# Seven-product quads: weight sums by accumulating transfers, seventeen quads, aligned operands

## The chip, the core and the metric

The program runs on one core of one Trainium2 chip. Its time is the device time in microseconds (us), the median of several runs. TensorE multiplies, ScalarE (ACT) and VectorE (DVE) work on elements, GpSimd (POOL) does a few small steps and can issue transfers, SyncE (SP) issues most transfers.

## What is computed

One layer of a hybrid block, on 256 rows of 2048 numbers in float32, with all the weights read from memory once:

```python
hn = rms_norm(x, norm_w)
proj = hn @ w_in                 # q, k, v, z_a, z_s, xbc, dt, g_a, g_s
o_a = dilated attention of q, k, v, times silu(z_a)
y = rms_norm(ssd scan of conv(xbc), times silu(z_s))      # 4096 wide
merged = sigmoid(g_a) * (o_a @ w_attn_branch) + sigmoid(g_s) * (y @ w_ssm_branch)
out = rms_norm(x + merged @ w_out)
```

The change touches two of these products: y @ w_ssm_branch (256 x 4096 by 4096 x 2048, called ssm) and the v part of hn @ w_in (256 x 2048 by 2048 x 2048, called v).

## The kernel before

Every product is made from two parts of each factor: a number is split into h, its value rounded to the matmul's format (ScalarE, a copy), and l, the rest (VectorE, a subtraction). Three matmuls xh*h, xh*l and xl*h are one full product; `triple` (lines 381 to 384) issues them. A matmul here has a 128 x 128 left block and 512 columns.

The weights lie in memory in the order of use, in units of 128 x 1024 numbers, 512 KB (`lay_weights`). SP loads a unit into one of four buffers w (`load`), ScalarE and VectorE split it into h and l, of which there are four buffers each (`unit`, lines 209 to 226), and TensorE multiplies. The tile framework sets the semaphores and, from a simulated timeline, the order on each engine and on SP's queue. A block under `high_priority(L_AHEAD)` is put ahead; loads are not in such a block. SP and POOL work their queues in order, and an instruction that waits for a buffer holds up what stands behind it.

The stages follow each other: the scan with its projections (pool ssm), then ssm and v (pool mul), then attention with q, k, za and the gates ga (pool att), then the attention branch and the output. ssm and v are made by `gemm_pair` (lines 373 to 449), each in two halves of 1024 columns (c = 0 and c = 2). A half runs over slots q of 256 rows of the weights: 16 in ssm, 8 in v. A plain slot multiplies 2 x 2 blocks of the left side with 2 x 2 blocks of the weights: 8 products, 24 matmuls. A *quad* (slots named in `S_QUADS`) makes the same from 7 products, 21 matmuls, in the manner of Strassen and Winograd: some products are of sums of blocks. For that the two units of a quad are laid out as (B11, B22) and (B12, B21). The seven are summed over all quads of a half in four extra PSUM banks, the prods; `fold` (lines 451 to 461) combines them, and they are added to the plain banks es. The second half swaps the roles of the eight banks.

In a quad VectorE makes t13 = (B12 - B11, B12 - B22) from both units (line 425), then two more sums in the place of B12 and B21 (lines 430 and 431). The parts of the units are named ha, la (of B11, B22) and hc, lc (of B21), those of the sums ht, lt (htt and ltt for t13, htu and ltu for the others in the profile). The left factors are sums too: `turn_x` (lines 351 to 364) adds h and l of a left block back together, makes four sums S and splits them into sx, 4 KB in each partition. It is called for all of ssm's quads before the first half (line 794), and the second half uses the same; for v it is called ahead of each half for the quads that are new.

The pools of SBUF are stacked: lead, big (the large left sides XT and yT), stream (w, h, l), ev (three pairs of 1 KB tiles for evacuating PSUM), const, and then one stage's pool after another at the same place. The pool mul now starts at byte 184192 of a partition, 384 past a multiple of 512. The memory of a stage's pool is free for the next when the last reader of what lay there is done.

Of the kernel before, what the change touches and what calls it, by code (L numbers as in the profile page):

```python
# [9 lines left out]
F32 = mybir.dt.float32  # L10
F32R = mybir.dt.float32r
AF = mybir.ActivationFunctionType
ALU = mybir.AluOpType
PSUM = bass.MemoryType.PSUM

P = 128
# [22 lines left out]
    ("ssm", 0): (3, 6, 9, 12), ("ssm", 2): (3, 6, 9, 12),  # L39
# [128 lines left out]
def hybrid_block(ctx: ExitStack, tc: tile.TileContext, wall, xt, x, pk_d, cst_d, fw_d, out):  # L168
# [6 lines left out]
    ev = ctx.enter_context(tc.tile_pool(name="ev", bufs=2))  # L175
# [175 lines left out]
    def turn_x(pool, x):  # L351

        sx = pool.tile([P, 2, 4, P], F32R, name=f"sx{now[0]}", tag="sx", bufs=4)
        tmp = pool.tile([P, 4, 512], F32, name=f"sxt{now[0]}", tag="tmp", bufs=1)
        a = tmp[:, 0].rearrange("p (k i s) -> p k i s", k=2, i=2)
        s = tmp[:, 1].rearrange("p (n s) -> p n s", n=4)
        xf = x.bitcast(F32)
        ve.tensor_tensor(a.rearrange("p k i s -> p k (i s)"), xf[:, :, :S], xf[:, :, S:], ALU.add)
        a11, a21, a12, a22 = a[:, 0, 0], a[:, 0, 1], a[:, 1, 0], a[:, 1, 1]
        ve.tensor_tensor(s[:, 0], a21, a22, ALU.add)  # L360
        ve.tensor_tensor(s[:, 1], a21, a11, ALU.subtract)
        ve.tensor_tensor(s[:, 2], s[:, 0], a11, ALU.subtract)
        ve.tensor_tensor(s[:, 3], a12, s[:, 2], ALU.subtract)
        split(s, sx[:, 0], sx[:, 1])
        return sx

    def gemm_pair(tag, pool, x_of, n_kt, sxs, swap, extra):

# [19 lines left out]
        for q in range(n_q):  # L388
# [32 lines left out]
            two = lambda t: t.rearrange("p (k m) -> p k m", k=2)  # L421
            with tc.high_priority(L_AHEAD):
                t13 = pool.tile([P, UNIT], F32, name=f"t13_{n}", tag="t13", bufs=1)
                b12 = wb[:, :512].unsqueeze(1).to_broadcast([P, 2, 512])
                ve.tensor_tensor(two(t13), b12, two(wa), ALU.subtract)
# [4 lines left out]
                ve.tensor_tensor(wb[:, :512], wa[:, 512:], t13[:, :512], ALU.subtract)  # L430
# [6 lines left out]
            sx = [(sx[:, 0, k], sx[:, 1, k]) for k in range(4)]  # L437
# [14 lines left out]
    def fold(prods, dst):  # L452

        d11, d12, d21, d22 = dst
        p1, p5, p6, p7 = prods
        ac.activation(d11, p1, AF.Copy)
        ac.activation(d22, p5, AF.Copy)
        ve.tensor_tensor(d12, p6, d11, ALU.add)
        ve.tensor_tensor(d21, p7, d12, ALU.add)
        ve.tensor_tensor(d12, d12, d22, ALU.add)  # L460
        ve.tensor_tensor(d22, d21, d22, ALU.add)
# [27 lines left out]
    rx = cpool.tile([P, S], F32, name="rx", tag="rx")  # L489
# [46 lines left out]
    dtT = cpool.tile([P, 2, SH], F32, name="dtT", tag="dtT")  # L536
    acT = cpool.tile([P, 2, SH], F32, name="acT", tag="acT")
    crT = cpool.tile([P, SH], F32, name="crT", tag="crT")
    acum_d = dram.tile([SH, S], F32, name="acum_d", tag="acum_d")

    with tc.tile_pool(name="ssm", bufs=2) as sp:
        def dt_sum(acc):
            hx, lx = dts[:, 6, :], dts[:, 7, :]
            ac.activation(hx, acc[:SH, S:], AF.Copy)
            ac.activation(lx, acc[SH:, :S], AF.Copy)
            ve.tensor_tensor(hx, acc[:SH, :S], hx, ALU.add)
            ve.tensor_tensor(hx, hx, lx, ALU.add)
# [159 lines left out]
        def find_r():  # L707
            part = cpool.tile([P, 4], F32, name="part", tag="part")
            for n in range(4):
                ac.activation(x_block(n), x_block(n), AF.Square, accum_out=part[:, n : n + 1])  # L710
            sums = cpool.tile([P, 2], F32, name="sums", tag="sums")
# [58 lines left out]
    with tc.tile_pool(name="mul", bufs=1) as sm:  # L770
        def scale_gate():
# [32 lines left out]
        sxs = {}  # L804
        for c in (0, 2):
            for q in S_QUADS[("v", c)]:
                if q not in sxs:
                    sxs[q] = turn_x(sm, XT[:, 2 * q : 2 * q + 2, :])
            es, prods = gemm_pair(("v", c), sm, lambda kt: XT[:, kt, :], KT, sxs, c == 2, {})
            dst = blocks(vt, c)  # L810
            fold(prods, dst)
            for d, e in zip(dst, es):
                ve.tensor_tensor(d, e, d, ALU.add)

    late = ctx.enter_context(tc.tile_pool(name="late", bufs=1))
    th_a = late.tile([P, 2, D], F32, name="th_a", tag="th_a")
    with tc.tile_pool(name="att", bufs=2) as ap:

# [145 lines left out]
```

## Time and profile before

| | us |
|---|---|
| median of 3 runs | 1409.14 (1409.02 to 1409.28) |
| the profiled execution | 1409.67 |
| its span, from the first to the last instruction | 1407.9 |
| ssm, from its first matmul to v's first | 586.0 to 756.7 |
| v, to the end of its last plain slot | 756.7 to 841.5 |
| TensorE busy in the span | 1395.6 |
| VectorE busy | 1005.2 |
| ScalarE busy | 782.6 |

How to read the rows below. A row of a timeline has start, duration, engine, line, operation, tiles written and read, form and count, and in brackets the idle time before it and what ended it. Matmuls are pipelined, so one starts before the one before it has ended: the step is the distance of two starts, not the duration. A row by stage has each engine's busy time and its count of instructions (those that overlap the edge are counted), then the granted clock, the share of the 16 DMA engines' time, and GB/s. A row on transfers has count, size of one, and median us from issue to landing. A row on waits has the total, the number of times and the longest.

### The profile page before, as it was taken

The numbers are of one execution on the slowest core, as the hardware profiler recorded it, in microseconds if no ns is written. First come the engines' busy times: TensorE is split into PE (matmuls) and PEld (weight loads), VectorE is DVE, ScalarE is ACT, GpSimd is POOL, SyncE is SP. The second block draws the span as 40 slices with busy tenths as digits, with TensorE's granted clock in tenths as the row PEclk, the third lists the DMA queues.
The fourth block names the chain that finished last, engine by engine and source line by source line (L and its number), as shares of the span: only waits on it lengthen the run. The fifth ranks groups of instructions, "written<-read, shape, count | busy, mean of one in ns | idle before, by whom it ended". The sixth has DMA issues, their size and how long they took to land.

```text
span 1407.9 us, 19734 instructions
## 1 busy us (share of the span) xinstructions
PE 1395.6 (99%) x7347; PEld 1184.9 (84%) x7347; DVE 1005.2 (71%) x1483; ACT 782.6 (56%) x1209; POOL 15.2 (1%) x66
## 2 busy tenths in 40 slices
PE   9999999999999999999999999999999999999997
PEld 7788888888888888888888888888888888888886
DVE  6988787776788797787777986666666654455654
ACT  7657577675668576665454554544444444444443
POOL 1000000000000000000000000000000000000000
PEclk9999999999999999999999999999999999999999
DMA  9666565656565665556556566555555557666663
GB/s 322 222 208 211 174 204 171 216 181 198 176 209 188 196 197 175 180 180 214 189 193 200 193 220 184 179 175 170 175 170 174 171 178 280 193 186 187 184 194 120
DMA packets 78208, 272.31 MB, mean 193 GB/s; under 512 B 8800, under 2 KB 9376, under 8 KB 77728
## 3 DMA queue, kind: packets, MB, share of 16 engines
q1 hardware_dynamic: 77392, 269.88, 60.9%
q8 instruction: 57, 0.93, 0.3%
q10 hardware_dynamic: 720, 1.18, 0.2%
q14 instruction: 39, 0.32, 0.1%
HBM read 268.86 MB, written 2.16 MB: 193 GB/s over the span
## 4 chain that ended last, share of the span: by engine, by line
PE 98%; DVE 1%; DMA 0%; SPq 0%; issue 0%; ACT 0%; POOLq 0%; DVEq 0%; POOL 0%
PE ps_zs L260 8%; PE ps_xs L260 8%; PE ps_za L260 4%; PE ps_k L260 4%; PE ps_q L260 4%; PE ps_zs L261 4%; PE ps_xs L261 4%; PE ps_ssm L382 4%; PE ps_ssm L383 4%; PE ps_ssm L384 3%; PE ps_q L261 2%; PE ps_k L261 2%; PE ps_za L261 2%; PE ps_attn L346 2%; PE ps_attn L347 2%; PE ps_attn L348 2%
## 5 line engine op out<-in xcount | busy, mean ns | idle before, releaser
L222 DVE TENSOR_TENSOR l<-w,h 128x1024 fp32r<-128x1024 f32 (+1 forms) x454 | 549.1, 1213 | 308.8 <-ACT h L221 306.0
L221 ACT ACTIVATE h<-w 128x1024 fp32r<-128x1024 f32 (+1 forms) x454 | 476.2, 1050 | 478.1 <-issue 92.5
L260 PE MATMUL ps_zs<-XT,h 128*128 128x512 f32 x496 | 176.2, 397 | 0.0
L260 PE MATMUL ps_xs<-XT,h 128*128 128x512 f32 x496 | 175.0, 395 | 0.0
L261 PE MATMUL ps_zs<-XT,l 128*128 128x256 f32 x496 | 139.4, 281 | 0.0
L261 PE MATMUL ps_xs<-XT,l 128*128 128x256 f32 x496 | 138.8, 280 | 0.0
L260 PEld LDWEIGHTS ps_zs<-XT,h 128*128 128x128 f32 x496 | 93.1, 188 | 22.7 <-issue 1.2
L260 PEld LDWEIGHTS ps_xs<-XT,h 128*128 128x128 f32 x496 | 93.0, 188 | 21.7
L261 PEld LDWEIGHTS ps_zs<-XT,l 128*128 128x128 f32 x496 | 93.6, 189 | 0.1
L261 PEld LDWEIGHTS ps_xs<-XT,l 128*128 128x128 f32 x496 | 93.6, 189 | 0.0
L260 PE MATMUL ps_q<-XT,h 128*128 128x512 f32 x256 | 92.3, 404 | 0.0
L260 PE MATMUL ps_za<-XT,h 128*128 128x512 f32 x256 | 89.6, 394 | 0.0
L260 PE MATMUL ps_k<-XT,h 128*128 128x512 f32 x256 | 89.6, 394 | 0.0
L383 PE MATMUL ps_ssm<-l,yT 128*128 128x512 f32 x192 | 74.9, 390 | 0.0
L384 PE MATMUL ps_ssm<-h,yT 128*128 128x512 f32 x192 | 74.6, 390 | 0.0
L382 PE MATMUL ps_ssm<-h,yT 128*128 128x512 f32 x192 | 72.4, 390 | 0.0
L261 PE MATMUL ps_q<-XT,l 128*128 128x256 f32 x256 | 71.2, 278 | 0.0
L261 PE MATMUL ps_za<-XT,l 128*128 128x256 f32 x256 | 71.0, 277 | 0.0
L261 PE MATMUL ps_k<-XT,l 128*128 128x256 f32 x256 | 71.0, 277 | 0.0
L260 PEld LDWEIGHTS ps_k<-XT,h 128*128 128x128 f32 x256 | 48.0, 188 | 11.2
L260 PEld LDWEIGHTS ps_za<-XT,h 128*128 128x128 f32 x256 | 48.0, 188 | 11.2
L260 PEld LDWEIGHTS ps_q<-XT,h 128*128 128x128 f32 x256 | 48.0, 188 | 10.9
(349 smaller groups left out, 2787.7 us busy)
## 6 DMA issues: line engine op xcount, KB each, us to landing
w<-in_wall SPq DMA_DIRECT2D x480, 512.0 KB, 3.7
acb<-acum_d SPq DMA_DIRECT2D x32, 256.0 KB, 3.6
th_s<-in_x SPq DMA_DIRECT2D x4, 512.0 KB, 7.5
fin<-in_x SPq DMA_DIRECT2D x1, 2048.0 KB, 9.4
early<-in_xt SPq DMA_DIRECT2D x7, 256.0 KB, 7.4
fw<-in_fw SPq DMA_DIRECT2D x1, 1024.0 KB, 11.5
out<-fin SPq DMA_DIRECT2D x4, 256.0 KB, 2.9
out<-fin ACTq DMA_DIRECT2D x4, 256.0 KB, 3.2
```

The costliest lines, as they stand in the source:

```text
L221: ac.activation(h[:, a:b], w[:, a:b], AF.Copy)
L222: ve.tensor_tensor(l[:, a:b], w[:, a:b], h[:, a:b].bitcast(F32), ALU.subtract)
L260: pe.matmul(acc, h[:, kk, :], m, start=(kt == 0), stop=False)
L261: pe.matmul(acc[:, S:], l[:, kk, :], m[:, :S], start=False, stop=(kt == KT - 1))
L346: pe.matmul(accs[i], xh, h, start=(kt == 0), stop=False)
L347: pe.matmul(accs[i], xh, l, start=False, stop=False)
L348: pe.matmul(accs[i], xl, h, start=False, stop=(kt == n_kt - 1))
L382: pe.matmul(acc, xh, h, start=start, stop=False)
L383: pe.matmul(acc, xh, l, start=False, stop=False)
L384: pe.matmul(acc, xl, h, start=False, stop=stop)
```

## The change

- ssm has quads at slots 3, 5, 7, 9, 11 and 13 rather than 3, 6, 9 and 12, in both halves; v keeps two and three. 17 quads rather than 13.
- The signs of the sums are turned so that t13 = (B12 + B11, B12 + B22). It is no longer made by VectorE: SP loads B12 into both halves of t13 (2 x 256 KB), and POOL issues a transfer of the unit (B11, B22) that adds to t13 as it lands (512 KB). The unit itself is loaded into w as before, of the second unit only the half B21. t13 has two buffers rather than one.
- In ssm the first S is kept in the left block that a quad no longer needs (A21), so sx has three sums, 3 KB, and six buffers; v keeps four sums and has three buffers. The factors get pools of their own, xp1 and then xp2 at the same place.
- The pool ev is gone: its tiles move into the scan's and the attention's pools, and the tiles rx, dtT, acT, crT, part and sums move from const into the scan's. A tile `line` of 448 bytes goes to the head of mul. What follows it starts at a multiple of 512 bytes.

```diff
 S_QUADS = {
-    ("ssm", 0): (3, 6, 9, 12), ("ssm", 2): (3, 6, 9, 12),
+    ("ssm", 0): (3, 5, 7, 9, 11, 13), ("ssm", 2): (3, 5, 7, 9, 11, 13),
...
-    ev = ctx.enter_context(tc.tile_pool(name="ev", bufs=2))
...
-    def turn_x(pool, x):
-
-        sx = pool.tile([P, 2, 4, P], F32R, name=f"sx{now[0]}", tag="sx", bufs=4)
-        tmp = pool.tile([P, 4, 512], F32, name=f"sxt{now[0]}", tag="tmp", bufs=1)
+    def turn_x(pool, temp, x, spare):
+
+
+        sx = pool.tile([P, 2, 4 - spare, P], F32R, name=f"sx{now[0]}", tag="sx", bufs=6 if spare else 3)
+        tmp = temp.tile([P, 4, 512], F32, name=f"sxt{now[0]}", tag="tmp", bufs=1)
...
-        ve.tensor_tensor(s[:, 0], a21, a22, ALU.add)
-        ve.tensor_tensor(s[:, 1], a21, a11, ALU.subtract)
+        ve.tensor_tensor(s[:, 0], a21, a22, ALU.subtract)
+        ve.tensor_tensor(s[:, 1], a11, a21, ALU.subtract)
         ve.tensor_tensor(s[:, 2], s[:, 0], a11, ALU.subtract)
-        ve.tensor_tensor(s[:, 3], a12, s[:, 2], ALU.subtract)
-        split(s, sx[:, 0], sx[:, 1])
-        return sx
+        ve.tensor_tensor(s[:, 3], a12, s[:, 2], ALU.add)
+        parts = [(sx[:, 0, n], sx[:, 1, n]) for n in range(4 - spare)]
+        if spare:
+            own = x[:, 0, P:S], x[:, 0, S + P :]
+            split(s[:, 0], *own)
+            parts.insert(0, own)
+        split(s[:, spare:], sx[:, 0], sx[:, 1])
+        return parts
...
-            for m in (n, n + 1):
-                if m not in loaded:
-                    load(m)
-            wa, wb = loaded.pop(n), loaded.pop(n + 1)
+
+            t13 = pool.tile([P, UNIT], F32, name=f"t13_{n}", tag="t13", bufs=2)
+            for c in range(2):
+                nc.sync.dma_start(t13[:, c * 512 : (c + 1) * 512], wall[n + 1, :, :512])
+            gp.dma_start(t13, wall[n], accum_op=ALU.add)
+            load(n)
+            wa = loaded.pop(n)
+            wb = stream.tile([P, UNIT], F32, name=f"w{n + 1}", tag="w", bufs=W_BUFS)
+            nc.sync.dma_start(wb[:, 512:], wall[n + 1, :, 512:])
...
             with tc.high_priority(L_AHEAD):
-                t13 = pool.tile([P, UNIT], F32, name=f"t13_{n}", tag="t13", bufs=1)
-                b12 = wb[:, :512].unsqueeze(1).to_broadcast([P, 2, 512])
-                ve.tensor_tensor(two(t13), b12, two(wa), ALU.subtract)
                 ha, la = hl(stream, "a", "hl", H_BUFS)
                 part(wa, ha, la)
                 hc, lc = hl(stream, "c", "hl", H_BUFS)
                 part(wb[:, 512:], hc[:, :512], lc[:, :512])
-                ve.tensor_tensor(wb[:, :512], wa[:, 512:], t13[:, :512], ALU.subtract)
-                ve.tensor_tensor(wb[:, 512:], wb[:, 512:], wb[:, :512], ALU.subtract)
+                ve.tensor_tensor(wb[:, :512], t13[:, 512:], wa[:, :512], ALU.add)
+                ve.tensor_tensor(wb[:, 512:], wb[:, :512], wb[:, 512:], ALU.add)
                 ht, lt = hl(pool, "t", ("ht", "lt"), 2)
                 part(t13, ht, lt)
...
-        ve.tensor_tensor(d12, d12, d22, ALU.add)
-        ve.tensor_tensor(d22, d21, d22, ALU.add)
+        ve.tensor_tensor(d12, d22, d12, ALU.subtract)
+        ve.tensor_tensor(d22, d22, d21, ALU.subtract)
...
-    rx = cpool.tile([P, S], F32, name="rx", tag="rx")
...
-    dtT = cpool.tile([P, 2, SH], F32, name="dtT", tag="dtT")
-    acT = cpool.tile([P, 2, SH], F32, name="acT", tag="acT")
-    crT = cpool.tile([P, SH], F32, name="crT", tag="crT")
...
     with tc.tile_pool(name="ssm", bufs=2) as sp:
+        ev = sp
+        rx = sp.tile([P, S], F32, name="rx", tag="rx", bufs=1)
+        dtT = sp.tile([P, 2, SH], F32, name="dtT", tag="dtT", bufs=1)
+        acT = sp.tile([P, 2, SH], F32, name="acT", tag="acT", bufs=1)
+        crT = sp.tile([P, SH], F32, name="crT", tag="crT", bufs=1)
...
     with tc.tile_pool(name="mul", bufs=1) as sm:
+        sm.tile([P, 112], F32, name="line", tag="line")
+
...
+        xpool = ExitStack()
+        xp = xpool.enter_context(tc.tile_pool(name="xp1", bufs=1))
         for c in (0, 2):
             if c == 0:
                 for q in S_QUADS[("ssm", c)]:
-                    sxs[q] = turn_x(sm, yT[q // 8][:, 2 * q % 16 : 2 * q % 16 + 2, :])
+                    sxs[q] = turn_x(xp, sm, yT[q // 8][:, 2 * q % 16 : 2 * q % 16 + 2, :], 1)
...
+        xpool.close()
+        xp = xpool.enter_context(tc.tile_pool(name="xp2", bufs=1))
         for c in (0, 2):
             for q in S_QUADS[("v", c)]:
                 if q not in sxs:
-                    sxs[q] = turn_x(sm, XT[:, 2 * q : 2 * q + 2, :])
+                    sxs[q] = turn_x(xp, sm, XT[:, 2 * q : 2 * q + 2, :], 0)
...
     with tc.tile_pool(name="att", bufs=2) as ap:
+        ev = ap
```

More of the change, by code (lines that the diff above doesn't have):

```diff
@@ L436, in gemm_pair @@
             sx = sxs[q]
-            sx = [(sx[:, 0, k], sx[:, 1, k]) for k in range(4)]
             lo, hi = slice(0, 512), slice(512, 1024)
@@ L707, in find_r @@
         def find_r():
-            part = cpool.tile([P, 4], F32, name="part", tag="part")
+            part = sp.tile([P, 4], F32, name="part", tag="part", bufs=1)
             for n in range(4):
                 ac.activation(x_block(n), x_block(n), AF.Square, accum_out=part[:, n : n + 1])
-            sums = cpool.tile([P, 2], F32, name="sums", tag="sums")
+            sums = sp.tile([P, 2], F32, name="sums", tag="sums", bufs=1)
             ve.tensor_tensor(sums, part[:, 0:4:2], part[:, 1:4:2], ALU.add)
@@ L813, in hybrid_block @@
                 ve.tensor_tensor(d, e, d, ALU.add)
+        xpool.close()
     late = ctx.enter_context(tc.tile_pool(name="late", bufs=1))
```

1 line of the change is left out of this document (removed).

## The prediction

> **What bounds the kernel now.** I read the page first (busy time, chain), then the busy time by stage, then TensorE and VectorE instruction by instruction around a quad, then the transfers and the waits. The page:
>
> ```profile
> span 1407.9 us, 19734 instructions
> ...
> PE 1395.6 (99%) x7347; PEld 1184.9 (84%) x7347; DVE 1005.2 (71%) x1483; ACT 782.6 (56%) x1209; POOL 15.2 (1%) x66
> ...
> PE 98%; DVE 1%; DMA 0%; SPq 0%; issue 0%; ACT 0%; POOLq 0%; DVEq 0%; POOL 0%
> ```
>
> TensorE is busy for 99% of the span and is 98% of the chain that ended last. So only two things can gain: fewer matmuls, or a shorter step from one to the next. Everything else can only hide or lose. The stages that the change touches (ssm from 586.0 to 756.7, v to 841.5), with the densest DMA stretch of the run as the last row:
>
> ```profile
> core 0: us, PE busy (x) PEld busy (x) DVE busy (x) ACT busy (x) POOL busy (x), PEclk, DMA share, GB/s
> 586.00:602.90 16.90, 16.90 (x79) 14.12 (x79) 15.56 (x26) 9.59 (x13) 0.83 (x1) 1.00 0.38 126
> ...
> 612.20:640.00 27.80, 27.80 (x123) 22.80 (x122) 26.63 (x36) 15.94 (x18) 0.00 (x0) 1.00 0.61 192
> 640.00:700.00 60.00, 60.00 (x265) 49.42 (x264) 45.22 (x48) 28.43 (x30) 0.00 (x0) 1.00 0.65 209
> ...
> 586.00:756.70 170.70, 170.70 (x752) 140.58 (x752) 133.56 (x158) 88.13 (x95) 2.02 (x1) 1.00 0.60 194
> ...
> 1172.00:1184.00 12.00, 12.00 (x55) 9.93 (x54) 4.35 (x5) 5.48 (x7) 0.00 (x0) 1.00 1.01 413
> ```
>
> TensorE has no idle time in any of them and the granted clock is 1.00. VectorE is the close second: 96% (26.63 of 27.80) while the left factors are turned, 75% (45.22 of 60.00) afterwards. The DMA engines have room: 0.65 of their time at 209 GB/s, and 413 GB/s when full, with TensorE still fed.
>
> **The change, part by part.** First the price of a quad. A plain slot is two units, 24 matmuls; a quad is 21. TensorE's timeline has both:
>
> ```profile
> 592.01 0.39 PE L384 MATMUL ps_ssm<-h,yT 128*128 128x512 f32 x1
> ...
> 597.45 0.39 PE L384 MATMUL ps_ssm<-h,yT 128*128 128x512 f32 x1
> ...
> 735.76 0.39 PE L382 MATMUL pp_ssm<-ha,yT 128*128 128x512 f32 x1
> ...
> 736.45 0.40 PE L382 MATMUL ps_ssm<-ha,sx 128*128 128x512 f32 x1
> ...
> 737.15 0.39 PE L382 MATMUL ps_ssm<-hc,yT 128*128 128x512 f32 x1
> ...
> 737.85 0.40 PE L382 MATMUL pp_ssm<-htt,sx 128*128 128x512 f32 x1
> ...
> 740.63 0.39 PE L382 MATMUL ps_ssm<-h,yT 128*128 128x512 f32 x1
> ```
>
> From 592.01 to 597.45 lie 24 matmuls: 5.44 us, 0.2267 each. From 735.76 to 740.63 lie the 21 of a quad: 4.87 us, 0.2319 each. A quad therefore saves 0.57 us. *Four more quads* (6+6 in ssm instead of 4+4): 4 x 0.57 = **-2.3 us**, on the path.
>
> *Operands at multiples of 512 bytes.* The pool of the multiplying stage starts 384 bytes past such a multiple now, so sx, t13, ht and lt do too, and 15 of a quad's 21 matmuls read one of them. Upper bound: all 21 run at the plain 0.2267, 4.87 - 4.76 = 0.11 us a quad, 17 quads, -1.9 us. Lower bound: nothing, because the aligned triples of the same quad are no faster: ha,yT took 0.69 and hc,yT 0.70, where ha,sx took 0.70. A loss is excluded by the operands' only moving to where the plain ones are. I take the middle, **-0.9 us**: neither row is nearer.
>
> *Sums by transfers.* One subtraction per quad leaves VectorE; two half loads on SP and one accumulating transfer on POOL's queue come; the later load of the half B12 goes. What VectorE does around the first quad, and how TensorE takes it:
>
> ```profile
> 594.04 0.69 DVE L679 TENSOR_TENSOR ssq<-ssq,xs 128x512 f32<-128x512 f32 x1
> ...
> 595.62 1.23 DVE L419 TENSOR_TENSOR la<-w,ha 128x1024 fp32r<-128x1024 f32 x1
> 596.76 1.22 DVE L425 TENSOR_TENSOR t<-w,w 128x1024 f32<-128x1024 f32 x1
> 597.90 0.68 DVE L358 TENSOR_TENSOR sxt<-yT 128x512 f32<-128x512 f32 x1
> 598.50 0.69 DVE L419 TENSOR_TENSOR lc<-w,hc 128x512 fp32r<-128x512 f32 x1
> 599.10 0.68 DVE L430 TENSOR_TENSOR w<-w,t 128x512 f32<-128x512 f32 x1
> 599.70 0.28 DVE L360 TENSOR_TENSOR sxt<-sxt 128x128 f32<-128x128 f32 x1
> 599.90 0.28 DVE L361 TENSOR_TENSOR sxt<-sxt 128x128 f32<-128x128 f32 x1
> ...
> 603.39 0.39 PE L382 MATMUL pp_ssm<-ha,yT 128*128 128x512 f32 x1
> ...
> 604.75 0.62 PE L382 MATMUL ps_ssm<-h,yT 128*128 128x512 f32 x2
> ...
> 607.27 0.39 PE L382 MATMUL pp_ssm<-htt,sx 128*128 128x512 f32 x1
> ```
>
> From start to start: 1.14 us for 1024 columns, 0.60 for 512, 0.20 for 128. A quad costs VectorE 4 x 1.14 + 3 x 0.60 = 6.36 now (la, t, ltt, ltu; lc and the two sums in w), 5.22 after. A plain slot is 2.28. A turned factor is 0.60 + 4 x 0.20 + 0.60 = 2.0; in ssm its split goes in two pieces (one S kept in x's unused block, which makes the 3 KB), so 2.2 by estimate, and six rather than four are turned in the first half. From 595.62 to the end of quad 13: 6 x 5.22 + 5 x 2.28 + 6 x 2.2 = 55.9 us of VectorE. TensorE takes slots 3 to 13 from 603.39 in 6 x 4.8 + 5 x 5.44 = 56 us, to 659.4. So VectorE has 63.8 us for 55.9, 88%: hidden, cost 0, by a cover of 7.9 us. The second half turns nothing. Saved VectorE time gains nothing.
>
> The transfers:
>
> ```profile
> w<-in_wall SPq DMA_DIRECT2D x63, 512.0 KB, 4.2
> ...
> w<-in_wall SPq DMA_DIRECT2D x2, 256.0 KB, 3.2
> ...
> fw<-in_fw SPq DMA_DIRECT2D x1, 1024.0 KB, 11.5
> ...
> w<-in_wall SPq DMA_DIRECT2D x21, 512.0 KB, 6.1
> ```
>
> (ssm; start; the full stretch; the first 60 us.) No accumulating transfer is in this trace. Its bounds from issue to landing: 3.2 (a plain half-size load) and 11.5 us (twice the bytes among full engines). I take 4.2, which has its size and its stage. Halves and accumulation make 7.4 us, at most 3.2 + 11.5 = 14.7. With two t13 buffers each serves every second quad: 4 slots, 20.5 us, less about 3.5 in use. So it is early in the steady state even at 14.7: cost 0.
>
> The first quad has no such lead. With ev, rx, dtT and the like moved into the ssm pool, t13 comes to lie where xs and zs were, whose last reader is the add at 594.04 to 594.73. Then 594.7 + 7.4 = 602.1, htt and ltt 2.2 more: 604.3. TensorE needs them after its first three triples, 603.39 + 9 x 0.23 = 605.5. Cost 0; at 14.7 it is 611.6, 6.1 us late, less what the next slot's matmuls can fill (those on h, from 604.75 on, stood in until 607.27 here).
>
> Moved along at no cost. SP issues four transfers per quad instead of two, and a half load that waits for its buffer holds up the w loads behind it; POOL's accumulation waits for both halves, and behind it stands only r_y, whose gate is used only when this half is folded. The folds' changed signs keep their number. The second half's prods end one slot later; its fold then has to leave the banks before v starts. The waits that say how much lead there is:
>
> ```profile
> ACT h L221 <- PE ps_ssm L384: 30.8, 23, 2.1
> ACT htt L418 <- DVE t L425: 25.8, 10, 4.7
> ...
> DVE t L425 <- DMA w<-in_wall: 12.1, 8, 2.4
> ...
> 744.51 0.69 DVE L461 TENSOR_TENSOR tmp<-tmp 128x512 f32<-128x512 f32 x1
> ```
>
> ScalarE waited 23 times for TensorE to free a buffer: the lead is full there. The fold ended at 745.2, 11.5 us before v at 756.7; one slot later leaves 6.
>
> **Sum:** -2.3 - 0.9 = -3.2 us. The profiled execution took 1409.67 us (span 1407.9 and 1.8 around it), 0.5 above the median of 1409.14: 1406.5 for it, **1405.9 us** for the median. An alignment worth nothing gives 1406.8, worth everything 1404.9. At the lowest every ssm matmul steps by 0.2267: the code has 24 x 24 + 8 x 21 = 744 of them, which would take 168.7 us of the 170.7, and 0.9 of that difference is the quads', counted already; the other 1.1 make 1403.8.
>
> On the accumulating transfer the Trainium skill ("SBUF — State Buffer", "SBUF: two separate sides") says that its descriptors are written by GpSimd, which a VectorE instruction in a two-port mode locks out, and ("Who interferes with whom") that tensor_tensor has no such mode. By the rule as stated the sum is unchanged, since the VectorE rows above are tensor_tensor. If every VectorE instruction did lock it out, each accumulation would start up to 1.2 us later: nothing in the steady state, and 604.3 becoming 605.5 at the first quad, still 1405.9. No run shows it yet.
>
> **The rivals.**
> *VectorE or the first t13 holds up the first half of ssm.* For: 15.56 of 16.90 us busy before the first quad, 96% later, and the cover is only 7.9 us for six quads; t13 may land at 609.4. Against: TensorE did not idle at that 96%. Price: between 0 and 6.1 us, middle 2.7: 1408.6, within 0.2% (which is 2.8 us, about what a measurement of this kernel can tell from no change).
> *The accumulation costs the DMA engines more than its bytes: slower.* Place: slots 3 to 13, every second one a quad. Plain transfers there: 5 x 1.05 + 6 x 1.31 = 13.1 MB, 31.8 us at 413 GB/s. Of 56 us 24 remain for six accumulations, 4.0 us of all 16 engines each, where 0.52 MB take 1.3 us as a plain copy. It decides from three times a copy's cost; at four times (5.1 us) each half loses 6 x 1.1 = 6.6 us: 1405.9 + 13.2 = 1419. For: nothing shows the rate of adding. Against: three times is a lot.
> *Late weights.* With 256 KB halves and POOL's packets between them, w lands after 6.1 us, as in the first 60 us, not 4.2. VectorE already waited 12.1 / 8 = 1.5 us for w before a quad; with w's four buffers held longer, 0.6 us lost in each of 12 quads gives 1413.1.
> *The change does less than it says*, alignment nothing: 1406.8, inside the first case.
>
> **Chances.** Sum holds: 0.54 (own range 1403.8 to 1406.9; 0.05 of it over 1406.3). First half held up: 0.24. Accumulation dear: 0.14. Late weights: 0.08. Faster by over 0.2%: 0.49; within: 0.05 + 0.24 = 0.29; slower: 0.14 + 0.08 = 0.22. The range 1403.8 to 1412.0 leaves out the last two, 0.22, which is near 2 in 10.
>
> **What would show it.** Right: ssm has 20 x 24 + 12 x 21 = 732 matmuls, not 744; the stretch from the first ps_ssm matmul to the first ps_v is some 2.8 us shorter; a quad takes 4.76 to 4.87; POOL's transfers land in 4 to 6 us, and no htt waits for one after the first. Wrong: idle TensorE time before htt or ltu in slots 3 to 13; VectorE near 100% there with TensorE waiting for l; a DMA share of 1.0 between quads; w landing in 6 us and more; or an aligned quad still at 0.232 a matmul.

## The result, and the profile after

The changed kernel takes **1423.97 us** (median; 1422.36 to 1424.61), the kernel before 1409.21 beside it: by the means of the runs 1.0102 times as long, 95% interval 1.0084 to 1.0119. It is 14.8 us slower, where 1405.9 was forecast with a range up to 1412.0. The profiled execution took 1423.43 us.

The page of the changed kernel, the lines that answer to those shown of before, with the two large DMA queues added (packets, MB, share of the 16 engines' span):

```profile
span 1421.6 us, 19917 instructions
...
PE 1397.1 (98%) x7335; PEld 1181.4 (83%) x7335; DVE 1007.0 (71%) x1504; ACT 789.3 (56%) x1225; POOL 29.0 (2%) x83
...
q1 hardware_dynamic: 82288, 274.34, 61.2%
q0 software_dynamic: 2448, 8.91, 3.5%
...
PE 87%; DMA 6%; DVE 4%; issue 1%; ACT 1%; SPq 0%; DVEq 0%; POOLq 0%; ACTq 0%; POOL 0%
```

TensorE was 98% of the chain that ended last and is 87%; DMA has gone from 0 to 6%, VectorE from 1 to 4%. Queue q0 is new: POOL's 17 accumulating transfers, 3.5% of the span for 8.91 MB.

By stage, in rows like those of before (engines' busy time, granted clock, share of the DMA engines, GB/s). First the changed kernel's ssm and v, then its first half of ssm around the quads:

```profile
587.80:770.30 182.50, 170.92 (x742) 137.43 (x742) 140.37 (x185) 96.54 (x112) 13.14 (x15) 1.00 0.80 240
770.30:854.40 84.10, 83.97 (x370) 69.08 (x369) 70.21 (x90) 43.69 (x49) 2.60 (x3) 1.00 0.76 233
...
605.00:660.00 55.00, 47.64 (x200) 36.42 (x198) 41.43 (x63) 31.32 (x37) 5.02 (x6) 1.00 0.87 251
```

From first matmul to first matmul ssm starts 1.8 us later (586.0 to 587.8), is 11.5 longer (171.0 to 182.5), v is 0.4 shorter, and what follows v is 0.8 longer (566.4 to 567.2). That is the 13.7 by which the span grew. (The table of before ends ssm at 756.7, where v's first block is loaded; v's first matmul starts at 757.0, so ssm took 171.0 and not 170.7.) In ssm TensorE is idle for 11.6 of 182.5 us, and of those 55 us around the first quads for 7.4, with VectorE busy for only 41.43 (75%). The DMA engines' share in those 55 us is 0.87, where it was 0.61 to 0.65 before.

Transfers from 605 to 660 us (queues, then count, size and median us from issue to landing):

```profile
q1 hardware_dynamic: 3958, 10.63, 54.7%
q0 software_dynamic: 864, 3.15, 31.8%
...
w<-in_wall SPq DMA_DIRECT2D x13, 512.0 KB, 6.2
t<-in_wall POOLq DMA_DIRECT2D x5, 512.0 KB, 8.3
t<-in_wall SPq DMA_DIRECT2D x10, 256.0 KB, 5.1
```

The adding queue moves 23% of the bytes (3.15 of 13.78 MB) in 37% of the time (31.8 of 86.5). A w load lands after 6.2 us; the prediction took 4.2 from ssm before.

How TensorE comes to wait, in one of these places. ScalarE's timeline, then one row of VectorE's with TensorE's, then some of the longest pieces of the chain there (start, us, what), then who waited for a w load, in ssm of after (the first two rows) and of before (us in all, times, longest):

```profile
630.48 1.04 ACT L220 ACTIVATE h<-w 128x1024 fp32r<-128x1024 f32 x1
635.12 1.06 ACT L220 ACTIVATE h<-w 128x1024 fp32r<-128x1024 f32 x1 [3.60 <-DMA w<-in_wall]
636.08 1.04 ACT L429 ACTIVATE htu<-w 128x1024 fp32r<-128x1024 f32 x1
```

```profile
631.20 0.68 DVE L438 TENSOR_TENSOR w<-w 128x512 f32<-128x512 f32 x1
...
633.55 0.84 PE L388 MATMUL ps_ssm<-h,yT 128*128 128x512 f32 x3
637.17 0.50 PE L388 MATMUL pp_ssm<-htu,sx 128*128 128x512 f32 x1 [2.78 <-ACT htu L429]
```

```profile
603.74 5.43 DMA t<-in_wall
...
617.60 5.58 DMA w<-in_wall
...
627.57 7.45 DMA w<-in_wall
```

```profile
ACT h L220 <- DMA w<-in_wall: 24.8, 14, 3.6
DVE w L437 <- DMA w<-in_wall: 15.8, 5, 5.1
...
ACT h L221 <- DMA w<-in_wall: 8.7, 6, 1.9
```

A w load issued at 627.57 landed at 635.0, 7.45 us later: POOL had issued an accumulating transfer at 626.35, which landed at 634.8. ScalarE stood at the split of that unit from 631.5 to 635.1. Behind it stood htu, whose operand VectorE had finished at 631.9. TensorE waited 2.78 us for htu. So a late w reaches TensorE in two ways, by its own h and by what is queued behind that h on ScalarE. VectorE adds a third: the two stalls of the second half (1.6 and 1.7 us, at 737 and 749) are waits for an l that stood behind a sum, and the sum had waited 5.1 and 4.1 us for its w.

Counted by steps of TensorE over 0.26 us, against the usual 0.227, the stalls in ssm come to 15.4 us (more than the 11.6 of idle time, since a matmul's modelled duration of 0.39 us reaches beyond its step): 4.5 at the first quad (609 to 618 us), where t13 itself was late, and the rest, but for 0.2 that before has as well, at later quads.

### The profile page after: what moved, and what is told of

Its sections match the earlier page's. It is cut to its first block, busy times and chain, and to the rows that moved or that the text cites. A ratio compares the mean times of both kernels' runs of the same rounds, so it can differ in the third digit from the quotient of the medians.

```text
span 1421.6 us, 19917 instructions
## 1 busy us (share of the span) xinstructions
PE 1397.1 (98%) x7335; PEld 1181.4 (83%) x7335; DVE 1007.0 (71%) x1504; ACT 789.3 (56%) x1225; POOL 29.0 (2%) x83
## 3 DMA queue, kind: packets, MB, share of 16 engines
q0 software_dynamic: 2448, 8.91, 3.5%
## 4 chain that ended last, share of the span: by engine, by line
PE 87%; DMA 6%; DVE 4%; issue 1%; ACT 1%; SPq 0%; DVEq 0%; POOLq 0%; ACTq 0%; POOL 0%
PE ps_zs L259 8%; PE ps_xs L259 8%; DMA w<-in_wall 6%; PE ps_k L259 4%; PE ps_za L259 4%; PE ps_q L259 4%; PE ps_zs L260 4%; PE ps_xs L260 4%; PE ps_q L260 2%; PE ps_za L260 2%; PE ps_k L260 2%; PE ps_attn L347 2%; PE ps_attn L346 2%; PE ps_ga L345 2%; PE ps_attn L345 2%; PE ps_out L346 2%
## 5 line engine op out<-in xcount | busy, mean ns | idle before, releaser
L221 DVE TENSOR_TENSOR l<-w,h 128x1024 fp32r<-128x1024 f32 (+1 forms) x446 | 539.3, 1213 | 308.3 <-ACT h L220 306.3
L220 ACT ACTIVATE h<-w 128x1024 fp32r<-128x1024 f32 (+1 forms) x446 | 467.6, 1050 | 486.5 <-issue 92.3
L389 PE MATMUL ps_ssm<-l,yT 128*128 128x512 f32 x160 | 62.8, 392 | 3.8 <-DVE l L221 3.8
L390 PE MATMUL ps_ssm<-h,yT 128*128 128x512 f32 x160 | 62.5, 390 | 0.0
L388 PE MATMUL ps_ssm<-h,yT 128*128 128x512 f32 x160 | 56.7, 392 | 0.9 <-ACT h L220 0.9
```

Source lines behind the costliest of these rows:

```text
L220: ac.activation(h[:, a:b], w[:, a:b], AF.Copy)
L221: ve.tensor_tensor(l[:, a:b], w[:, a:b], h[:, a:b].bitcast(F32), ALU.subtract)
L388: pe.matmul(acc, xh, h, start=start, stop=False)
L389: pe.matmul(acc, xh, l, start=False, stop=False)
L390: pe.matmul(acc, xl, h, start=False, stop=stop)
```

## Experiments

Thirteen kernels. "After" is the changed kernel; each ratio is of the means, against the kernel before, run beside it (median 1409.2 for after, 1409.5 to 1409.9 for the others).

| kernel | us | ratio, 95% interval |
|---|---|---|
| after | 1423.97 | 1.0102 [1.0084, 1.0119] |
| e1: after, quads of ssm as before | 1415.04 | 1.0037 [1.0023, 1.0052] |
| e2: after, t13 by VectorE | 1409.75 | 1.0001 [0.9992, 1.0010] |
| e3: e2, operands at 384 past 512 | 1412.55 | 1.0019 [1.0010, 1.0029] |
| e4: after, plain copy for the adding | 1411.91 | 1.0016 [1.0006, 1.0025] |
| e5: before, tiles moved | 1412.43 | 1.0019 [1.0010, 1.0028] |
| e6: e2, other tiles at their old places | 1406.95 | 0.9981 [0.9973, 0.9990] |
| e7: after, t13's transfers a slot earlier in the code | 1424.10 | 1.0102 [1.0086, 1.0117] |
| e8: e6, 5 + 6 quads in ssm | 1406.31 | 0.9976 [0.9966, 0.9986] |
| e9: before, ev's tiles 32 bytes on | 1409.68 | 1.0001 [0.9991, 1.0010] |
| e10: before, operands aligned | 1407.44 | 0.9983 [0.9975, 0.9992] |
| e11: e8, ssm pool at multiples of 64 | **1404.96** | **0.9967 [0.9954, 0.9979]** |
| e12: e10, ssm pool's tiles 64 bytes back | 1409.61 | 1.0000 [0.9990, 1.0009] |
| e13: after, 5 + 5 quads in ssm | 1413.72 | 1.0031 [1.0022, 1.0041] |

### The adding, the copies, the quads and the alignment (e1 to e4)

The theories: A, adding is dear for the DMA engines; B, the chain from the half loads over the adding to the sums is too long; C, VectorE and the w buffers are held too densely by a quad in every second slot. e1:

```diff
-    ("ssm", 0): (3, 5, 7, 9, 11, 13), ("ssm", 2): (3, 5, 7, 9, 11, 13),
+    ("ssm", 0): (3, 6, 9, 12), ("ssm", 2): (3, 6, 9, 12),
```

> The changed kernel with the old 13 quads (ssm 3, 6, 9, 12 in both halves), everything else as changed: the sums still come by transfers. Three theories for the 14.8 us lost. A, the adding is dear: an adding 4 KB packet takes 328 ns of a DMA engine where a plain one takes 159, and what is loaded beside it lands late; then the loss falls about with the number of ssm quads, 8 instead of 12, and more because of the plain slot that is added between them: 1410 to 1416. B, the chain of halves, addition and VectorE's sums holds the w buffers too long at every quad: 1412 to 1418. C, quads at every second slot are too dense for VectorE and the four w buffers, whoever makes the sums: near 1408 (13 quads, aligned, sums off VectorE).

e2, where VectorE makes t13 again, by the new signs as a sum:

```diff
-            t13 = pool.tile([P, UNIT], F32, name=f"t13_{n}", tag="t13", bufs=2)
-            for c in range(2):
-                nc.sync.dma_start(t13[:, c * 512 : (c + 1) * 512], wall[n + 1, :, :512])
-            gp.dma_start(t13, wall[n], accum_op=ALU.add)
-            load(n)
-            wa = loaded.pop(n)
-            wb = stream.tile([P, UNIT], F32, name=f"w{n + 1}", tag="w", bufs=W_BUFS)
-            nc.sync.dma_start(wb[:, 512:], wall[n + 1, :, 512:])
+            for m in (n, n + 1):
+                if m not in loaded:
+                    load(m)
+            wa, wb = loaded.pop(n), loaded.pop(n + 1)
...
+                b12 = wb[:, :512].unsqueeze(1).to_broadcast([P, 2, 512])
+                ve.tensor_tensor(two(t13), b12, two(wa), ALU.add)
```

> The changed kernel with its 17 quads, pools and alignment, but t13 is made by VectorE from the two loaded units again: no half loads, no transfer on POOL's queue. A and B: the weights come in time again, TensorE does not wait in ssm: 1404 to 1407 (-2.3 us for four quads, 0 to -1.9 for the alignment). C: VectorE has 6 x 6.36 + 5 x 2.28 + 13.2 = 62.8 us of work for 63.8 us in the first half and is late: 1410 to 1424.

e3 is e2 with `line` 32 columns shorter, so that sx, t13, ht and lt begin at 384 past a multiple of 512 bytes:

```diff
-        sm.tile([P, 112], F32, name="line", tag="line")
+        sm.tile([P, 80], F32, name="line", tag="line")
```

> As e2_vector_sum, but the tile at the head of mul is 320 bytes instead of 448, so that sx, t13, ht and lt start 384 bytes past a multiple of 512, as in the kernel before. If the alignment is worth what the steps of quad matmuls show (389 ns a matmul in the changed kernel, 393 to 404 before), it is 1 to 2 us slower than e2_vector_sum, and its quads' matmuls last 393 to 404 ns again; if the longer matmuls had another cause, the same within 0.3 us.

e4 is the changed kernel without the addition (it leaves B12 out of t13, so it doesn't compute the product):

```diff
-            gp.dma_start(t13, wall[n], accum_op=ALU.add)
+            gp.dma_start(t13, wall[n])
```

> The changed kernel, but POOL's transfer copies the unit over t13 and does not add; it still waits for the two half loads, and is as large. It leaves out the addition, so t13 lacks B12 and the quads' products are not those of the reference. A: a packet takes 159 ns again, six transfers per half free 6 x 1.4 us of all DMA engines, w lands in 5 us rather than 6 to 8, and most of the loss goes: 1407 to 1413. B or C: the same chain and the same bytes from memory, 1420 to 1424.

Measured: with t13 made by VectorE the time is 1409.75, so the transfers for t13 cost 14.2 us more than VectorE's sums. With the same transfers as plain copies it is 1411.91: copies for sums cost 2.2 us, and the adding 12.1 more. The page of e4 has POOL's queue, and its transfers from 605 to 660 us, beside those shown above:

```profile
q0 software_dynamic: 2448, 8.91, 1.8%
...
w<-in_wall SPq DMA_DIRECT2D x15, 512.0 KB, 5.1
...
t<-in_wall POOLq DMA_DIRECT2D x5, 512.0 KB, 5.5
```

The same packets and bytes take 1.8% of e4's span of 1408.7 us and 3.5% of 1421.6 with the adding: 1.49 and 2.93 us of all 16 engines for each of the 17 transfers, twice as much. The transfer lands after 5.5 rather than 8.3 us, and a w after 5.1 rather than 6.2. In ssm ScalarE waits for w 6.8 us in all, 1.7 at the longest, rather than 24.8 and 3.6. That is theory A.

In e1, with a quad in every third slot, all stalls of TensorE (steps over 0.26 us) lie at the first quad, 609 to 618 us, 4.7 us together (but for the 0.2 of before); the later seven cost nothing. So from the second quad on the adding is hidden at one quad in three, and with after's six at one in two it is not.

e3 against e2 is 2.8 us: the alignment. Two of TensorE's groups in ssm, of e3 and then of e2:

```profile
L388 PE MATMUL ps_ssm<-ha,sx 128*128 128x512 f32 x12 | 4.9, 408 | 0.0
L388 PE MATMUL pp_ssm<-htt,yT 128*128 128x512 f32 x12 | 4.7, 395 | 0.0
```

```profile
L388 PE MATMUL ps_ssm<-ha,sx 128*128 128x512 f32 x12 | 4.8, 399 | 0.1
L388 PE MATMUL pp_ssm<-htt,yT 128*128 128x512 f32 x12 | 4.7, 390 | 0.0
```

Moved by 128 bytes, the groups of a quad's matmuls last 389 to 408 ns instead of 389 to 399 (htu,yT aside, which had also waited in both). The mean step, without stalls, is 0.2324 us for those that read sx, ht or lt, instead of 0.2270.

### Is it the lead? (e7)

```diff
             ks = [x_of(2 * q + k) for k in range(2)]
+            if q + 1 in quads:
+                m = first + 2 * q + 2
+                t = t13s[q + 1] = pool.tile([P, UNIT], F32, name=f"t13_{m}", tag="t13", bufs=2)
+                for c in range(2):
+                    nc.sync.dma_start(t[:, c * 512 : (c + 1) * 512], wall[m + 1, :, :512])
+                gp.dma_start(t, wall[m], accum_op=ALU.add)
```

> The changed kernel, where a quad's two half loads and its accumulating transfer are issued one slot (5.4 us) earlier than its other weights; nothing else. Theory A, the adding fills the DMA engines (a 4 KB packet 328 ns where a plain one takes 159): the work of the engines is the same, so the share near the first quads stays at about 0.87, w lands after 6 us as now, and the time stays at 1420 to 1424. Theory B, the chain of half load, adding and sums is only too long for the lead it gets: the t13 buffers are filled 5.4 us sooner, htu and ltu no longer wait for it, and the time falls to what the plain copy in its place gave, 1411 to 1413.

Measured 1424.10, as after. The row of 605 to 660 us:

```profile
605.00:660.00 55.00, 49.03 (x198) 38.31 (x197) 41.38 (x64) 30.61 (x36) 4.87 (x6) 0.94 0.86 247
```

But nothing was issued earlier. Two of POOL's issues for t13, in after and then in e7:

```profile
626.35 0.89 POOL L417 DMA_DIRECT2D t<-in_wall  x1 [9.12 <-DVE w L437]
638.03 0.87 POOL L417 DMA_DIRECT2D t<-in_wall  x1 [10.79 <-DVE sxt L361]
```

```profile
626.58 0.89 POOL L404 DMA_DIRECT2D t<-in_wall  x1 [9.03 <-DVE w L440]
638.73 0.88 POOL L404 DMA_DIRECT2D t<-in_wall  x1 [11.26 <-DVE sxt L361]
```

The half loads wait for one of the two t13 buffers: VectorE's ltt ends at 620.92 in after and they go out at 620.95, at 621.14 and 621.16 in e7. So the edit gave no lead, and its time says nothing about theory B. The trace of after does. From the second quad of ssm on t13 landed at least 2.7 us before ScalarE split it, and VectorE's sum waited for it only once more (1.9 us at 710, with no stall of TensorE there). So from the second quad on the sums were not late, the weights beside them were; at the first quad t13 was late as well.

### By itself, or only at this pace? (e13)

```diff
-    ("ssm", 0): (3, 5, 7, 9, 11, 13), ("ssm", 2): (3, 5, 7, 9, 11, 13),
+    ("ssm", 0): (4, 6, 8, 10, 12), ("ssm", 2): (4, 6, 8, 10, 12),
```

> The changed kernel with its accumulating transfers, and five quads (4, 6, 8, 10, 12) in each half of ssm instead of six (3 to 13). In the first half VectorE turns five factors instead of six and the first quad stands one slot (5.4 us) later, so VectorE has some 48 us of work from the first factor to the last quad for 64; the spacing of the quads, and with it the DMA engines' work in each slot, stays. Theory 'adding by itself': the DMA engines stay at 0.85 and more around the quads, w still lands after 6 us, the stalls per quad stay: some 9 us in the first half and 3 in the second, 1420 to 1422. Rival 'only where VectorE has no room': VectorE makes up for late weights, the first half stalls 1 to 4 us, the second 3 as now, and the time is 1412 to 1416.

```profile
605.00:660.00 55.00, 52.52 (x227) 41.86 (x226) 43.29 (x65) 30.84 (x37) 4.40 (x5) 1.00 0.86 237
```

The median is 1413.72 (1411.44 to 1417.13), in the rival's range, though not by its parts: in the profiled execution, the slowest of the ten, the first half still stalls some 6 us (and 2 more at a halved clock, shown at the end), where 1 to 4 were expected, and the second, with five quads at one in two, not at all, where 3 were. The share is 0.86 as in after, so the loss is no fixed price of an adding transfer. Two quads fewer and a first quad one slot later take away 10 of the 14 us. But the rival's reason isn't shown either: VectorE was busy for 75% of these 55 us in after, 79% here. How much of the 10 us is the later start and how much the shorter run of quads, over which deficits add up, stays open.

### The time outside ssm and v (e5, e6, e9, e12)

Every variant so far reached ssm 1.4 to 2.4 us late, in an unchanged order of TensorE's work. e5 is the kernel before with the moved tiles alone:

```diff
-    ev = ctx.enter_context(tc.tile_pool(name="ev", bufs=2))
...
-    rx = cpool.tile([P, S], F32, name="rx", tag="rx")
...
     with tc.tile_pool(name="ssm", bufs=2) as sp:
+        ev = sp
+        rx = sp.tile([P, S], F32, name="rx", tag="rx", bufs=1)
+        dtT = sp.tile([P, 2, SH], F32, name="dtT", tag="dtT", bufs=1)
...
     with tc.tile_pool(name="att", bufs=2) as ap:
+        ev = ap
...
     with tc.tile_pool(name="mul", bufs=1) as sm:
+        sm.tile([P, 80], F32, name="line", tag="line")
```

> The kernel before with one part of the change alone: ev's tiles, rx, dtT, acT, crT, part and sums lie in the ssm pool (and ev's in att later); quads, sums and left factors as before, and the multiplying pool at the same 384 past a multiple of 512 bytes as before. Every variant of the changed kernel so far reached ssm 1.4 to 2.2 us later than before (587.4 to 588.2 against 586.0) and took 0.8 us longer after v. Theory 'places': the moved tiles alone do that: ssm starts at 587.4 to 588.2, the stretch from q to the end is 0.8 longer, the time is 1411.2 to 1412.2. Rival 'not the places' (another part of the change, or the order in which things are issued, does it): ssm starts at 586.0 and the time is 1409.2.

e6 is e2 with t13 in one buffer, ev as a pool of its own again and pads that put the tiles of all other stages back where they were:

```diff
+    ev = ctx.enter_context(tc.tile_pool(name="ev", bufs=2))
     cpool = ctx.enter_context(tc.tile_pool(name="const", bufs=1))
...
-        ev = sp
+        sp.tile([P, 16], F32, name="edge", tag="edge", bufs=1)
...
-        sm.tile([P, 112], F32, name="line", tag="line")
...
+    late.tile([P, 608], F32, name="edge2", tag="edge2")
```

> The changed kernel with its 17 quads, 3 KB left factors and operands at multiples of 512 bytes, but t13 made by VectorE (one buffer), and every tile outside ssm and v at the address it had before (ev is its own pool; rx, dtT, acT, crT, part and sums stand at the head of the ssm pool; hr lies in the lead pool). Theory 'places': ssm starts at 586.0, ssm takes 169.2 and v 83.6 as with VectorE's sums before, the stretch after v 566.4: together 1405.2 of span, 1406.5 to 1407.0 of time, 0.998 of before. Rival 'not the places': 1409 to 1410, as VectorE's sums without this gave (1409.75).

e5 took 1412.43 (+2.6), e6 1406.95 (2.8 under e2): the moved tiles cost that much, and the rival falls. Which tiles? e9 moves ev's alone, to 352 past a multiple of 512:

```diff
-    ev = ctx.enter_context(tc.tile_pool(name="ev", bufs=2))
...
+    ev = ctx.enter_context(tc.tile_pool(name="ev", bufs=2))
+    ev.tile([P, 8], F32, name="edge", tag="edge", bufs=1)
     with tc.tile_pool(name="ssm", bufs=2) as sp:
```

> The kernel before with one thing moved: ev's tiles (lo, th and the tiles that conv and zs work in) begin 32 bytes past a multiple of 64 (352 past a multiple of 512), where they began at multiples of 512; rx, dtT, acT and crT keep their place modulo 512, and the ssm, multiplying and att pools keep their addresses. Moving all of these together cost 2.6 us (1412.43 against 1409.85). Theory 'ev': reading and writing the evacuation's tiles at 32 past 64 makes the 512-wide matmuls of the projections slower by some 2 ns each, so ssm starts at 587.5 to 588, q to the end is 0.8 longer, and the time is 1412.0 to 1412.5. Rival 'rx, dtT, acT, crT or the ssm pool's own tiles': nothing moves, 1409.8.

Nothing (1409.68; its profiled execution was 2 us longer than its median). e12 moves the ssm pool's own tiles by 64 bytes, in the kernel e10 below:

```diff
-        part = sp.tile([P, 4], F32, name="part", tag="part", bufs=1)
-        sums = sp.tile([P, 2], F32, name="sums", tag="sums", bufs=1)
...
+            part = sp.tile([P, 4], F32, name="part", tag="part", bufs=1)
...
+            sums = sp.tile([P, 2], F32, name="sums", tag="sums", bufs=1)
```

> The run with aligned operands alone (13 quads, 1407.44 us), with the ssm pool's own tiles raw, xs, zs, bt, ct and cb 64 bytes further back, at the same places modulo 512 as in the changed kernel; ev's tiles and all else stay. Theory 'the ssm pool's tiles': the projections' 512-wide matmuls are 2 ns slower each, ssm starts at 587.4 to 588 instead of 585.7, and the time is 1409 to 1409.7. Rival 'ev's tiles at 416 and 480 past a multiple of 512': nothing moves, 1407.4.

1409.61 against 1407.44: 2.2 us, and the reading 'ev' is out. In the trace of e12 ssm starts at 588.3, in that of e10 at 585.7; the stretch after v is the same in both (566.4 and 566.3), so the 0.8 us there in after should come from other tiles (attention's begin at 64 rather than 384 past a multiple of 512); that wasn't tried. TensorE's groups from 60 to 580 us, of e10, of e12, and of e11 (below):

```profile
L259 PE MATMUL ps_zs<-XT,h 128*128 128x512 f32 x496 | 176.2, 397 | 0.0
L259 PE MATMUL ps_xs<-XT,h 128*128 128x512 f32 x496 | 175.0, 395 | 0.0
```

```profile
L259 PE MATMUL ps_zs<-XT,h 128*128 128x512 f32 x496 | 177.0, 399 | 0.0
L259 PE MATMUL ps_xs<-XT,h 128*128 128x512 f32 x496 | 176.1, 397 | 0.0
```

```profile
L260 PE MATMUL ps_zs<-XT,h 128*128 128x512 f32 x496 | 175.7, 395 | 0.0
L260 PE MATMUL ps_xs<-XT,h 128*128 128x512 f32 x496 | 174.3, 393 | 0.0
```

Neither operand of these matmuls has moved. What moved are the tiles that VectorE and ScalarE work on beside them, and the matmuls change by 2 ns each.

### The alignment and the quads alone, and the best version (e10, e8, e11)

e10 is the kernel before with its multiplying pool at byte 181760 rather than 184192:

```diff
-    rx = cpool.tile([P, S], F32, name="rx", tag="rx")
...
     with tc.tile_pool(name="ssm", bufs=2) as sp:
+        sp.tile([P, 16], F32, name="edge", tag="edge", bufs=1)
+        rx = sp.tile([P, S], F32, name="rx", tag="rx", bufs=1)
...
+    late.tile([P, 608], F32, name="edge2", tag="edge2")
```

> The kernel before with one part of the change alone: the multiplying pool begins at a multiple of 512 bytes (181760) instead of 384 past one; 13 quads, sums by VectorE, left factors in 4 KB, and every tile outside ssm and v at its old place. Theory 'alignment': the 15 matmuls of a quad that read sx, t13's or the sums' factors go from 393 to 404 ns long to 389, 0.17 us a quad as the two runs with VectorE's sums showed (2.8 us over 17 quads): 13 x 0.17 = 2.2 us, 1407.6; v takes 83.6 instead of 84.6. As the prediction had it: 0.9 x 13/17 = 0.7 us, 1409.1. The four quads are then worth the difference to the run with the places kept and 17 quads (1406.95): 0.7 us, less than their 2.3.

1407.44: 2.3 us for 13 quads. From there to e6's 17 quads are only 0.5 us, for 12 matmuls fewer (732, not 744; 2.7 us at 0.2267). The rest is given back in the first half of ssm, where e6 has VectorE busy for 98% of its time and TensorE short of work for 1.2 us in 55:

```profile
605.00:660.00 55.00, 53.80 (x235) 43.62 (x234) 54.15 (x81) 35.48 (x43) 0.00 (x0) 1.00 0.59 190
```

e8 has five quads there and six in the second half:

```diff
-    ("ssm", 0): (3, 5, 7, 9, 11, 13), ("ssm", 2): (3, 5, 7, 9, 11, 13),
+    ("ssm", 0): (4, 6, 8, 10, 12), ("ssm", 2): (2, 4, 6, 8, 10, 12),
...
+                extra[13] = lambda: sxs.update({2: turn_x(xp, sm, yT[0][:, 4:6, :], 1)})
```

> As the run with the places kept, but five quads (4, 6, 8, 10, 12) in the first half of ssm and six (2, 4, 6, 8, 10, 12) in the second, where quad 2's left factor is turned late in the first half: 16 quads in all. With six quads in the first half VectorE has 62.8 us of work for some 63.8 and TensorE stalled 2.2 us in three places. Theory C, VectorE's density costs those 2.2 us: they go, one quad of 0.57 us is lost, and the time is 1405.0 to 1405.5 if the places hold as well, 1.6 us below the run with 17 quads. Rival: the stalls come from the w buffers that a quad holds and not from VectorE's density: they stay, and this is 0.5 us above the run with 17 quads.

1406.31: one quad fewer and still 0.6 faster. The stalls fall from 2.2 to 0.8 us (steps over 0.26 us, in ssm and v). Theory C holds for VectorE's sums, at a smaller size than expected: 0.6 us gained, not 1.6. VectorE's work and the first quad's place both changed here; what each gave isn't separated. e11 puts the ssm pool's tiles at multiples of 64 bytes:

```diff
-        sp.tile([P, 16], F32, name="edge", tag="edge", bufs=1)
...
-            raw = sp.tile([P, 260], F32, name=f"raw_{name}", tag="raw", bufs=3)
+            raw = sp.tile([P, 272], F32, name=f"raw_{name}", tag="raw", bufs=3)
...
+            raw = raw[:, :260]
```

> The run with 16 quads and the places kept, with the ssm pool's tiles (raw, xs, zs, bt, ct, cb, gt, acb, xdt, y1) at multiples of 64 bytes, where most began 32 past one; raw is 12 columns longer for that, and part and sums stand beside half. Theory 'any tile at 32 past 64 that VectorE or ScalarE works on costs': the 512-wide matmuls of the projections fall by up to another 2 ns each, ssm starts some 1 to 2 us earlier than 586.0, and the time is 1404.5 to 1405.5. Rival 'only ev's tiles matter': 1406.3, as with 16 quads and the places kept.

1404.96, 4.8 us faster than before and the best of all. Its ssm starts at 584.6 rather than 586.0, and its rows of ssm and v:

```profile
584.60:752.90 168.30, 168.10 (x744) 138.74 (x744) 148.80 (x193) 95.04 (x109) 2.02 (x1) 1.00 0.62 197
752.90:836.60 83.70, 83.70 (x371) 69.28 (x371) 75.28 (x95) 44.70 (x49) 0.00 (x0) 1.00 0.63 200
```

## The prediction, step by step

The medians make a chain: from before to e6 -2.9 us (1409.85 to 1406.95: alignment, four quads and their stalls), to e2 +2.8 (moved tiles), to e4 +2.2 (copies in place of VectorE's sums), to after +12.1 (the adding). Together +14.2, where +14.8 was measured directly; before itself stood between 1409.2 and 1409.9.

- **What bounds the kernel** was right: TensorE's steps, with VectorE second. e6 and e8 move as this says.
- **Four more quads, -2.3 us.** The matmuls went (2.7 us of them), but with VectorE's sums 2.2 us came back as stalls, and 0.5 was left. VectorE's 88% was not what limited the changed kernel (75% busy around the first quads). With the sum for t13 it is 98%.
- **Alignment, -0.9 us** of 0 to -1.9, the middle. The size was off: 2.3 us for 13 quads, 2.8 for 17, 0.17 a quad, beyond the upper bound. As that bound had it, all 21 steps of a quad fall to 0.2267: from 0.2326 where they read sx, from 0.2333 for ht and lt (means of the steps under 0.26 us in ssm and v, before against e10). The triples on ha and hc, whose operands didn't move, fall as well, from 0.2305; that they were no faster than the others had been the lower bound's reason. Outside the bound lay the 846 plain steps, which go from 0.2264 to 0.2256, 0.7 us together. Why steps that read nothing moved get shorter stays open.
- **Moved tiles.** The sum has no term for their new places, and they cost 2.6 us (e5). Nothing in the trace of before shows the price.
- **Sums by transfers, cost 0.** This is the step that failed. Its bounds held: the accumulating transfer landed after 8.3 us (3.2 to 11.5 were given, 4.2 taken), halves and adding made 13.4 of at most 14.7, and as said no htt waited for t13 after the first quad (one wait of 5.5 us in all). The conclusion from them was wrong, since it asked only whether t13 comes in time. In place of 0 the adding cost 12.1 us and the copies for it 2.2 (e4). Of the 15.4 us of stalls 4.5 came at the first quad, where t13 was late; most of the rest is in the weights that share the engines with it, for which ScalarE waited 24.8 us in ssm rather than 8.7.
- **The first quad.** 602.1 was forecast, 609.4 at the worst; the transfer landed at 609.17 (the piece of 5.43 us from 603.74). SP reached its halves only at 597.37, 2.7 us later than assumed, and they landed at 600.85 and 603.09. So the chain started later and was shorter than at the worst, and that the two times agree is chance. TensorE's stalls from 609 to 618 come to 4.5 us, between the 0 to 6.1 given: to this size the rival "first half held up" (0.24) came true as well. One part had been costed at nothing, the gate that waits for r_y (4.08 us on ScalarE, at 605.07 before). r_y stood behind the accumulations on POOL (605.46 to 606.50), and the gate behind htt on ScalarE, which waited for t13. It began at 611.30 and put ha off to 615.27. TensorE waited for ha for 1.2 us.
- **The rival "accumulation dear", 0.14,** is nearest to what happened, with the rival "late weights" (0.08) as its way: w lands after 6.2 us, where that rival said 6.1. Its price of 0.6 us a quad was too low; the stalls behind the first quad come to 10.7 us for 11 quads, 1.0 each. The first rival's edge was put too high. An adding transfer costs 2.0 times a copy, and the text had it decide from three times. That edge came from 413 GB/s, a row of another stage. The row of ssm shown beside it, 209 GB/s at 0.65, gives 322 when full: 13.1 MB take 40.7 of the 56 us, six accumulations have 15.3, or 2.6 us each, and each took 2.93. By that row it decides below two copies, and its chance should have been far larger. This too is not the whole: the share was 0.87 and not 1, and in that window the plain queue's 10.63 MB took 54.7% of 55 us, which gives 353 GB/s when full and again an edge above two copies. My reading, which no run isolates, is that queueing was enough: four w buffers and a ScalarE that takes its work in order didn't cover landings of 6.2 to 7.5 us instead of 4.2.
- **The Trainium skill** on POOL being locked out ("SBUF — State Buffer", "SBUF: two separate sides") was weighed without effect on the sum, and POOL's issue of an accumulation took 0.86 to 1.05 us each time in after, so no wait of up to 1.2 us shows in it; the other side, a VectorE instruction in a two-port mode beside it, no run here shows.

## What to carry to other kernels

Work that moves from an engine to a transfer wasn't free in a stage that already filled two thirds of the DMA engines: count the new transfer's engine time at the rate of that same stage, allow an adding transfer twice a copy, and ask what becomes of the loads beside it, not only whether its own result comes in time. Relief is worth only what the relieved engine was costing: VectorE's sums cost 2.2 us of stalls here, and their replacement 15.4. And a change of layout is a change: moving tiles cost 2.6 us and aligning them gained 2.3, both the size of the arithmetic that was to be saved, so each is to be run by itself. And an experiment that is to issue something earlier tells nothing until its trace shows that it was issued earlier.

## What the runs showed of the hardware

- An accumulating transfer of 512 KB took 2.93 us of all 16 DMA engines (mean of 17 in after), the same as a plain copy 1.49 (e4).
- With the multiplying pool at 384 past a multiple of 512 bytes a quad's matmuls that read it step by 0.2326 to 0.2333 us, at a multiple of 512 by 0.2267, and ssm and v together take 2.3 us longer with 13 quads (before against e10). Whether it is TensorE's operand that counts isn't shown: VectorE's and ScalarE's tiles there moved too, and triples with no operand in that pool changed as well (0.2305 to 0.2267).
- TensorE's step depends on where other engines' tiles lie. With the ssm pool's tiles 64 bytes further back (e12) the projections' matmuls are 2 ns slower, at multiples of 64 (e11) 2 ns faster, with no operand of theirs moved. The Trainium skill ("SBUF — State Buffer", "Who interferes with whom") says that TensorE never waits on anyone for the memory; these runs differ from it, if a longer step counts as waiting, by 2.2 us for e12. What in the memory is shared isn't shown.
- After an idle stretch the clock can halve for a while. In the profiled execution of e13 TensorE waits and then steps by 0.43 us instead of 0.23, with a granted clock of 0.50 from 663.4 to 666.8:

```profile
660.79 0.39 PE L390 MATMUL ps_ssm<-h,yT 128*128 128x512 f32 x1
663.18 1.46 PE L388 MATMUL ps_ssm<-h,yT 128*128 128x512 f32 x3 [2.00 <-ACT h L220]
664.44 0.63 PE L388 MATMUL pp_ssm<-htu,sx 128*128 128x512 f32 x1
664.87 0.63 PE L388 MATMUL ps_ssm<-htu,yT 128*128 128x512 f32 x1
```

  That adds some 2 us to that execution, and the same came in e7 (granted clock 0.94 in its row), in a wait of 3.25 us. In after a step of 3.2 us at 634.0 had no such sequel. The Trainium skill ("TensorE: Matmul & The Clock Gate", "What's actually happening") has the clock halve after an idle window of about 3.4 us that runs free; here 2.0 us of idle time was enough once.
